# Attention scores: the low part of q against K's high part alone, as two 64-row matmuls on the two halves of the array

## The chip, the cores and the metric

The kernel runs on one core of a Trainium2 chip. The metric is the device time of one execution in microseconds (us). A profile of one execution goes with it: the hardware profiler's records of every instruction on TensorE (PE, and PEld for its weight loads), VectorE (DVE), ScalarE (ACT), GpSimd (POOL) and the queue of DMA issues on SyncE (SP).

## What is computed

The reference is a trunk of two layers over 2048 frames of width 1024: a gated MLP layer (A), then a chunked attention layer (B). The change touches the scores of layer B alone:

```
q, z = split(h @ w_qz);  q = q * 64 ** -0.5         # 16 heads of 64
for each chunk c of 64 queries:                      # keys: its own chunk and 8 before it
    sc = einsum('bqhd,bkhd->bhqk', qc, kc) + bias
    p  = softmax(where(valid, sc, -1e30))
    o  = einsum('bhqk,bkhd->bqhd', p, vc)
x = x + (o * silu(z)) @ w_out
```

## The kernel before

**Numbers in two parts.** TensorE takes the operands in a 32-bit form that it rounds (`F32R`). The kernel keeps the accuracy by writing every operand as a high part plus a low part and adding up products of parts. `mm3` (lines 113 to 116) does this for all projections with three matmuls: high by high (line 114), high by low (115), low by high (116). Each adds 128 rows of contraction into 512 columns.

**Scores.** A head is 64 wide, half of the array's 128 rows, and the kernel before uses the other half for the low part of K. `project(t, p)` makes, for each of the two heads `hd` of a pair `p`, a tile `kx` of 128 partitions and 1024 key columns. Its half `r` holds K's high part (ACT copy, line 1410), its other half `r2` K's low part (DVE subtraction, line 1411). The right 512 columns are the keys of the present stretch `t`. They are stored to `khd` in DRAM (line 1419), and the left 512, the keys of the stretch before, are loaded from there (line 1421). For q there are two tiles, `Qh` (high) and `Ql` (low), each made on one half of the partitions (lines 1397, 1398) and copied to the other half by a DMA (line 1403), so that both halves hold the same values.

`score(t, p, u)` takes 128 queries of one head (`u` counts eight such blocks of a pair, four for each head) against 640 keys, in two segments of 320 columns, each in a PSUM bank of its own. It issues four matmuls of 128 rows (line 1473): `Qh` with segment 0 and segment 1 of `kx`, then `Ql` with both. With `Qh` on both halves the sum over 128 rows is qh·kh + qh·kl, with `Ql` it is ql·kh + ql·kl. In the first stretch, t = 0, there are fewer keys and one segment only.

**Behind a score** come DVE (bias and row minimum, line 1481), ACT (exponential, 1488), DVE (reciprocal, 1491), POOL (scaling, 1492), then `flip`: five transposes on PE (1508), and the split of their result on ACT and DVE (1512, 1513). `value` multiplies by V (1533). `drain` adds the two halves of its result: ACT copies one half into the tile `ot` (1552), DVE adds the other (1553).

**Order.** The sequence is 2048 frames in four stretches `t` of 512, each with eight pairs of heads. In the loop over `u` the scores run two blocks ahead of `flip`; the generator `ahead` feeds in the projections of the next pair (tiles `pj`: q, then k, then the gate) and, from t = 1 on, the output projection of the stretch before (`bo`). What stands in the code is the order of issue that the author asks for. The framework's planner then arranges the instructions of each engine by its own estimates of when operands will be there; `add_manual_dep` (as in `on_beat`, `paced_by_pj`) ties some to others. So an engine's order in the trace need not be that of the code, and DMA issues on SP above all move.

**Buffers.** `ot` has a tag of its own with one buffer. The tag `C` has four buffers of 512 columns: in t = 1, for p below 4, `o_sums` takes four at a time for sums of output weights (tiles `wo`); from t = 1 on the output projection takes them for rows of the residual (`or`, `oc`, `jk`).

Of the kernel before, what the change touches and what calls it, by code (L numbers as in the profile page):

```python
# [9 lines left out]
F32 = mybir.dt.float32  # L10
F32R = mybir.dt.float32r
# [6 lines left out]
P = 128  # L18
# [3 lines left out]
T = 512  # L22
# [11 lines left out]
def trunk_kernel(  # L34
# [20 lines left out]
    nc = tc.nc  # L55
# [15 lines left out]
    khd = [  # L71
        [dram.tile([2, P, T], F32, name=f"khd{t}_{p}") for p in range(NPAIR)]
        for t in range(NT - 1)
    ]
# [163 lines left out]
    def keep_all():  # L238
        while kept:
            nc.sync.dma_start(*kept.pop(0))  # L240
# [1113 lines left out]
    with ExitStack() as bctx:  # L1354
        cb = bctx.enter_context(tc.tile_pool(name="cb", bufs=1, reuse_waits="tile"))
        sb = bctx.enter_context(tc.tile_pool(name="sb", bufs=2, reuse_waits="tile"))
# [5 lines left out]

        vtl = {}
        kt = {}
        qt = {}
        zt = {}

        def halves(hd):
            return slice(hd * 64, hd * 64 + 64), slice(64 - hd * 64, 128 - hd * 64)

        def half_tile(tag, name, bufs, dtype=F32):
            return sb.tile([P, 512], dtype, tag=tag, name=name, bufs=bufs)
# [17 lines left out]
        def project(t, p):  # L1390
            for acc in one(t, p, 1):
                yield
            for hd in range(2):
                qh = sb.tile([P, T], F32R, tag="Q", name=f"Qh{t}_{p}_{hd}", bufs=8)
                ql = sb.tile([P, T], F32R, tag="Q", name=f"Ql{t}_{p}_{hd}", bufs=8)
                r, r2 = halves(hd)
                nc.scalar.mul(qh[r, :], acc[r, :], 0.125)
                nc.vector.scalar_tensor_tensor(
                    ql[r, :], acc[r, :], 0.125, qh[r, :].bitcast(F32),
                    op0=ALU.mult, op1=ALU.subtract,  # L1400
                )
                for x_ in (qh, ql):
                    nc.sync.dma_start(x_[r2, :].bitcast(F32), x_[r, :].bitcast(F32))
                qt[t, p, hd] = (qh, ql)
            for acc in one(t, p, 0):
                yield
            for hd in range(2):
                r, r2 = halves(hd)
                kx = sb.tile([P, 2 * T], F32R, tag="K", name=f"K{t}_{p}_{hd}", bufs=4)
                nc.scalar.copy(kx[r, T:], acc[r, :])  # L1410
                nc.vector.tensor_tensor(
                    kx[r2, T:], acc[r, :], kx[r, T:].bitcast(F32), op=ALU.subtract
                )
                if t + 1 < NT:
                    k_store = (khd[t][p][hd], kx[:, T:].bitcast(F32))
                    if held:
                        kept.append(k_store)
                    else:
                        nc.sync.dma_start(*k_store)
                if t > 0:  # L1420
                    nc.sync.dma_start(kx[:, :T].bitcast(F32), khd[t - 1][p][hd])
                kt[t, p, hd] = kx
            if not held:
                keep_all()
# [33 lines left out]
        def score(t, p, u):  # L1458

            hd, qb = divmod(u, 4)  # L1460
            h = 2 * p + hd
            if qb == 1 and (h + 1 < NH or t + 1 < NT):
                load_bias(t + (h + 1) // NH, (h + 1) % NH)
            bias = bias_t[t, h]
            kx = kt[t, p, hd]
            c0 = 0 if t > 0 else 512 - qb * P
            n = 640 - c0
            koff = qb * P + c0
            ps = pss.tile([P, 2, 512], F32, tag="ss", name=f"s{t}_{h}_{qb}")
            nseg, w = (2, 320) if n == 640 else (1, n)  # L1470
            for i, q in enumerate(qt[t, p, hd]):
                for sg in range(nseg):
                    mm(  # L1473
                        ps[:, sg, :w], q[:, qb * P : (qb + 1) * P],
                        kx[:, koff + sg * w : koff + (sg + 1) * w],
                        start=i == 0, stop=i == 1,
                    )
            pr = sb.tile([P, 640], F32, tag="Pr", name=f"pr{t}_{h}_{qb}", bufs=4)
            ns = sm.tile([P, 2], F32, tag="ns", name=f"ns{t}_{h}_{qb}", bufs=4)
            nm, sl = ns[:, 0:1], ns[:, 1:2]  # L1480
            nc.vector.tensor_tensor_reduce(  # L1481
                out=pr[:, c0:].rearrange("p (a b) -> p a b", a=nseg),
                in0=ps[:, :nseg, :w],
                in1=bias[:, c0:].rearrange("p (a b) -> p a b", a=nseg),
                scale=-1.0, scalar=3.0e38, op0=ALU.add, op1=ALU.min,
                accum_out=nm,
            )
            nc.scalar.activation(  # L1488
                pr[:, c0:], pr[:, c0:], AF.Exp, scale=-1.0, bias=nm, accum_out=sl
            )  # L1490
            nc.vector.reciprocal(sl, sl)  # L1491
            nc.gpsimd.tensor_scalar(  # L1492
                pr[:, c0:], pr[:, c0:], sl, 1.0, op0=ALU.mult, op1=ALU.mult
            )
            prs[t, h, qb] = pr
# [49 lines left out]
        def drain(t, p, hd, po):  # L1545
            h = 2 * p + hd
            if hd == 0:
                og32s[t, p] = sb.tile([P, T], F32, tag="og32", name=f"og32_{t}_{p}", bufs=2)
            og32 = og32s[t, p]
            r, r2 = halves(hd)  # L1550
            ot = sb.tile([P, T], F32, tag="ot", name=f"ot{t}_{h}", bufs=1)
            nc.scalar.copy(ot[r, :], po[r2, :])
            nc.vector.tensor_tensor(og32[r, :], po[r, :], ot[r, :], op=ALU.add)
            if hd == 0:
                return
            if hd == 1 and t + 1 == NT and p >= 6:
                last_og(p, og32, zt[t, p])
            elif hd == 1:
                og = sb.tile([P, T], F32, tag="og", name=f"og{t}_{p}", bufs=2)
                nc.vector.scalar_tensor_tensor(  # L1560
                    og[:], og32[:], 0.5, zt[t, p][:], op0=ALU.mult, op1=ALU.mult
                )
                o4 = og[:].rearrange("p (j r s) -> p r j s", j=2, r=2)
                for r_ in range(2):
                    nc.sync.dma_start(ogd[t][:, r_, p], o4[:, r_])
# [383 lines left out]
        def steps_of(t, p):  # L1949
            n = 24  # L1950
            if p + 1 < NPAIR:
                n = 16 + 8 * len(GATES[t][p])
            elif t + 1 == NT:
                n = 13
            return n + SHARE[t][p]
# [12 lines left out]
        for t in range(NT):  # L1968
            for p in range(NPAIR):
                gen = ahead(t, p) if t + p else first  # L1970
                total = steps_of(t, p) - (0 if t + p else 8)
                per = 11 if p + 1 == NPAIR and t + 1 < NT else 16
                todo = []
                if t + 1 == NT and p + 1 == NPAIR:
                    o_early[t - 1, 3] = o_right(t - 1)(3)
                    todo = last_open()
                if t == 1 and p < 4:
                    todo = o_sums(p, lambda n: half_tile("C", n, 4), lambda n: half_tile(
                        "S", n, 4, F32R
                    ))  # L1980
                if (t, p) == (0, 3):
                    nc.sync.dma_start(gf[:], fin_g.partition_broadcast(P))
                done = 0
                for u in range(8):
                    if u < 6:
                        score(t, p, u + 2)
                    elif p + 1 < NPAIR or t + 1 < NT:
                        score(t + (p + 1) // NPAIR, (p + 1) % NPAIR, u - 6)
                    upto = total * (2 * u + 1) // per
                    take(gen, upto - done)  # L1990
                    done = max(done, upto)
                    if u == 4:
                        value(t, p, 0)
                    elif u == 0 and before:
                        value(*before, 1)
                    flip(t, p, u)
                    drain_all()
                    send_all()
                    square_all()
                    if u and finals:  # L2000
                        finals.pop(0)()
                    if todo:
                        todo.pop(0)()
                    upto = total * (2 * u + 2) // per
                    take(gen, upto - done)
                    done = max(done, upto)
                if t + 1 < NT or p + 1 < NPAIR:
                    run(gen)
                before = t, p
# [62 lines left out]
```

## Time and profile before

| | us |
|---|---|
| median of 3 runs | 2642.36 |
| lowest and highest | 2638.15, 2643.76 |
| the profiled execution, its own time | 2642.95 |
| its span (first to last instruction) | 2641.2 |
| first score matmul | 1527.6 after the start |

How to read it: a row of grouped instructions gives line, engine, operation, the tile written and those read, the shape, the count, then after the bar the time in which at least one was running, the mean duration in ns of one, and the idle time of the engine ahead of them with what ended it. A `LDWEIGHTS` puts the stationary operand into the array, a `MATMUL` streams the moving one. Matmuls are pipelined: the record of one lasts longer than the distance to the next, so rates are read from starts, not from durations. A row of the timeline gives start, duration, engine, line, operation, tiles, shape and how many like it follow each other.

### The profile page before, as it was taken

Reading aid. Unit: us, or ns where it says so; the run is one execution under the profiler, and the core shown is the slowest. Engines: PE = TensorE matmul, PEld = TensorE weight load, DVE = VectorE, ACT = ScalarE, POOL = GpSimd, SP = SyncE. Lnnn points to the kernel's source line nnn. Section 1 sums busy time; section 2 is a strip of 40 time slices with the busy share of each in tenths; the row PEclk is TensorE's granted clock in tenths of the full one; section 3 lists DMA queues with packets and bytes.
Section 4 is the critical chain, followed back from the end, with each engine's and each line's share of the span. In section 5 each row is a group of like instructions: output and inputs, shape, how many; then the busy total and the mean of one; then the engine's idle time right before and its main releaser. Section 6 shows DMA issues by size and latency. Waiting matters only on the chain. (4 is left out here: it accounts for less than half of the span.)

```text
span 2641.2 us, 37945 instructions
## 1 busy us (share of the span) xinstructions
PE 2583.6 (98%) x12752; PEld 2154.9 (82%) x12752; DVE 1933.1 (73%) x3040; ACT 1411.7 (53%) x2511; POOL 901.8 (34%) x875
## 2 busy tenths in 40 slices
PE   9999999999999999999989999999999999999997
PEld 7788788778888888888878778888888888888886
DVE  5984796776768667757776767778778777877677
ACT  7553373553644535333355456666656655666564
POOL 3802254152252413104134334344332322332245
PEclk9999999999999999999999999999999999999999
DMA  8899978988888869858776587778787666775667
GB/s 315 292 349 339 367 270 337 325 304 311 316 333 300 318 225 339 320 199 283 259 263 211 188 270 234 229 241 266 247 277 261 222 208 218 255 228 160 195 229 248
DMA packets 276162, 709.82 MB, mean 269 GB/s; under 512 B 29184, under 2 KB 69120, under 8 KB 275968
## 3 DMA queue, kind: packets, MB, share of 16 engines
q1 hardware_dynamic: 275968, 707.40, 77.6%
q8 instruction: 102, 1.67, 0.2%
q14 instruction: 92, 0.75, 0.1%
HBM read 520.11 MB, written 176.69 MB: 264 GB/s over the span
## 5 line engine op out<-in xcount | busy, mean ns | idle before, releaser
L114 PE MATMUL P<-T,S 128*128 128x512 f32 x1248 | 494.6, 396 | 14.1 <-DVE x L597 6.7
L116 PE MATMUL P<-T,S 128*128 128x512 f32 x1248 | 487.8, 391 | 0.0
L115 PE MATMUL P<-T,S 128*128 128x512 f32 x1248 | 487.3, 390 | 0.3 <-DVE T L522 0.3
L1492 POOL TENSOR_SCALAR pr<-pr,ns 128x640 f32<-128x640 f32 (+4 forms) x256 | 206.8, 808 | 534.2 <-DVE ns L1491 445.9
L114 PE MATMUL pj<-hh_b,wh_b 128*128 128x512 f32 x768 | 319.7, 416 | 0.2 <-ACT wh_b L231 0.2
L116 PE MATMUL pj<-hh_b,wl_b 128*128 128x512 f32 x768 | 303.8, 396 | 0.8 <-DVE wl_b L232 0.8
L115 PE MATMUL pj<-hl_b,wh_b 128*128 128x512 f32 x768 | 302.5, 394 | 0.0
L1488 ACT ACTIVATE pr<-pr,ns 128x640 f32<-128x640 f32 (+4 forms) x256 | 195.5, 764 | 194.6 <-DVE ns L1481 193.7
L114 PEld LDWEIGHTS P<-T,S 128*128 128x128 f32 x1248 | 234.6, 188 | 65.2 <-DVE x L597 6.2
L116 PEld LDWEIGHTS P<-T,S 128*128 128x128 f32 x1248 | 234.6, 188 | 50.8 <-DVE S L441 0.4
L115 PEld LDWEIGHTS P<-T,S 128*128 128x128 f32 x1248 | 234.9, 188 | 44.7 <-DVE T L522 0.6
L1513 DVE TENSOR_TENSOR pt<-tp,pt 128x640 fp32r<-128x640 f32 (+4 forms) x256 | 188.3, 736 | 43.9 <-ACT pt L1512 41.3
L1481 DVE CUSTOM_DVE_ANT_0 pr<-s,bias 128x640 f32<-128x640 f32 (+4 forms) x256 | 187.9, 734 | 36.2 <-PE s L1473 29.7
L1512 ACT CAST pt<-tp 128x640 fp32r<-128x640 f32 (+4 forms) x256 | 158.7, 620 | 53.7 <-PE tp L1508 49.6
L1508 PE MATMUL tp<-ident,pr 128*128 128x128 f32 x1120 | 166.6, 275 | 10.7 <-DVE pt L1513 8.2
L116 PEld LDWEIGHTS pj<-hh_b,wl_b 128*128 128x128 f32 x768 | 144.5, 188 | 35.4 <-DVE wl_b L232 2.9
L1508 PEld LDWEIGHTS tp<-ident,pr 128*128 128x128 f32 x1120 | 130.5, 141 | 46.1 <-issue 17.5
L114 PEld LDWEIGHTS pj<-hh_b,wh_b 128*128 128x128 f32 x768 | 145.4, 189 | 18.1 <-ACT wh_b L231 1.8
L1533 PEld LDWEIGHTS pv<-pt,V 128*128 128x128 f32 x896 | 142.8, 188 | 21.2 <-DVE pt L1513 4.5
L115 PEld LDWEIGHTS pj<-hl_b,wh_b 128*128 128x128 f32 x768 | 145.4, 189 | 16.2 <-DVE hl_b L189 0.2
L1533 PE MATMUL pv<-pt,V 128*128 128x256 f32 (+3 forms) x896 | 154.2, 319 | 2.4 <-DVE pt L1513 1.2
L232 DVE TENSOR_TENSOR wl_b<-raw_b,wh_b 128x1024 fp32r<-128x1024 f32 x96 | 120.5, 1257 | 28.8 <-ACT wh_b L231 27.9
(300 smaller groups left out, 5855.7 us busy)
## 6 DMA issues: line engine op xcount, KB each, us to landing
S<-hsd SPq DMA_DIRECT2D x224, 512.0 KB, 5.7
rw<-in_w_a SPq DMA_DIRECT2D x108, 512.0 KB, 6.3
A<-ytd SPq DMA_DIRECT2D x72, 512.0 KB, 5.8
raw_b<-wk SPq DMA_DIRECT2D x72, 512.0 KB, 4.2
hsd<-S SPq DMA_DIRECT2D x56, 512.0 KB, 6.0
V<-vhd SPq DMA_DIRECT2D x56, 512.0 KB, 5.5
bias<-reld SPq DMA_DIRECT2D x64, 320.0 KB, 4.1
va<-vd SPq DMA_DIRECT2D x32, 512.0 KB, 6.2
```

The lines of the kernel that those rows point to most:

```text
L114: first = mm(ps, lh, rh, start=first, stop=False)
L115: mm(ps, lh, rl, start=False, stop=False)
L116: mm(ps, ll, rh, start=False, stop=last)
L232: tv(wl[:], raw[:], wh[:].bitcast(F32), op=sub)
L1481: nc.vector.tensor_tensor_reduce(out=pr[:, c0:].rearrange("p (a b) -> p a b", a=nseg), in0=ps[:, :nseg, :w], in1=bias[:, c0:].rearrange("p ...
L1488: nc.scalar.activation(pr[:, c0:], pr[:, c0:], AF.Exp, scale=-1.0, bias=nm, accum_out=sl)
L1492: nc.gpsimd.tensor_scalar(pr[:, c0:], pr[:, c0:], sl, 1.0, op0=ALU.mult, op1=ALU.mult)
L1508: ins = tpose(tp[:, b, :], pr[:, b * P : (b + 1) * P], ident[:])
L1512: nc.scalar.copy(oh, tp[:, b0:5, :].rearrange("p a b -> p (a b)"))
L1513: nc.vector.tensor_tensor(pt[:, 2560 + o + b0 * P : 2560 + o + 640], tp[:, b0:5, :].rearrange("p a b -> p (a b)"), oh.bitcast(F32), op=ALU ...
L1533: mm(po[:, q0 * P : q1 * P], vtl[t, p][:, i, hs], rhs, start=(i == blocks[0] and j == 0), stop=(i == 7 and j == 1),)
```

## The change

`Ql` meets only K's high part: the product ql·kl is dropped, and the contraction of the `Ql` matmuls goes from 128 rows to 64. For t above 0, segment 0 runs on the half `r` of the array, where `kx` holds the high part, and segment 1 on the half `r2`. For that a second tile `K2` (one buffer for the whole kernel; head 0 uses one half of its partitions, head 1 the other) gets K's high part copied to the half `r2`, by two DMAs for each head: one from `kx`, one from `khd`. For head 0 they are issued in `project`, for head 1 at the start of the next pair's loop. `Qh` is as before, and so is t = 0. To make room, `ot` goes into the tag `C`.

```
         k2t = {}
         k2s = []
         second = []
...
                 if t > 0:
                     nc.sync.dma_start(kx[:, :T].bitcast(F32), khd[t - 1][p][hd])
+                    if not k2s:
+                        k2s.append(sb.tile([P, 2 * T], F32R, name="K2", bufs=1))
+                    k2 = k2t[t, p] = k2s[0]
+
+                    def again(k2=k2, kx=kx, r=r, r2=r2, src=khd[t - 1][p][hd]):
+                        nc.sync.dma_start(k2[r2, T:].bitcast(F32), kx[r, T:].bitcast(F32))
+                        nc.sync.dma_start(k2[r2, :T].bitcast(F32), src[r])
+
+                    if hd:
+                        second.append(again)
+                    else:
+                        again()
...
             for i, q in enumerate(qt[t, p, hd]):
                 for sg in range(nseg):
+                    rows, src = slice(0, P), kx
+                    if i and t > 0:
+                        rows, src = halves(hd)[sg], (kx, k2t[t, p])[sg]
                     mm(
-                        ps[:, sg, :w], q[:, qb * P : (qb + 1) * P],
-                        kx[:, koff + sg * w : koff + (sg + 1) * w],
+                        ps[:, sg, :w], q[rows, qb * P : (qb + 1) * P],
+                        src[rows, koff + sg * w : koff + (sg + 1) * w],
                         start=i == 0, stop=i == 1,
                     )
...
-            ot = sb.tile([P, T], F32, tag="ot", name=f"ot{t}_{h}", bufs=1)
+            ot = sb.tile([P, T], F32, tag="C", name=f"ot{t}_{h}", bufs=4)
...
                 done = 0
+                while second:
+                    second.pop(0)()
                 for u in range(8):
```

More of the change, by code (lines that the diff above doesn't have):

```diff
@@ L1364, in trunk_kernel @@
         kt = {}
+        k2t = {}
+        k2s = []
+        second = []
         qt = {}
```

## The prediction

> **What bounds the kernel now.** I read the page first: the busy shares, then the chain of waits that ended last.
>
> ```profile
> span 2641.2 us, 37945 instructions
> PE 2583.6 (98%) x12752; PEld 2154.9 (82%) x12752; DVE 1933.1 (73%) x3040; ACT 1411.7 (53%) x2511; POOL 901.8 (34%) x875
> PE 33%; DVE 5%; DMA 2%; issue 1%; POOL 1%; ACT 1%; SPq 0%; DVEq 0%; POOLq 0%; ACTq 0%
> PE pj L116 6%; PE pj L114 6%; PE pj L115 6%; PE pv L1533 5%; PE s L1473 4%; PE tp L1508 4%; PE bo L115 1%; PE bo L116 1%; PE bo L114 1%; DVE pt L1513 1%; DVE pr L1481 1%; DVE y L1831 1%; DVE wl_b L232 0%; DMA or<-x1d 0%; POOL raw_b L216 0%
> ```
>
> The chain accounts for 43% of the span, roughly the attention stage, which fills the last 1113 us. In it 33 of 43 parts are PE, and the scores (s L1473) have 4%, some 106 us. The view of windows confirms this for the three stretches t = 1, 2, 3; its columns after the length are busy time and count for PE, PEld, DVE, ACT and POOL, then clock, DMA share and GB/s.
>
> ```profile
> 1725.00:2012.00 287.00, 285.61 (x1566) 244.52 (x1565) 224.55 (x403) 185.48 (x333) 108.29 (x132) 1.00 0.80 263
> 2012.00:2303.00 291.00, 288.33 (x1579) 247.01 (x1578) 220.33 (x398) 177.15 (x317) 86.46 (x119) 1.00 0.70 226
> 2303.00:2590.00 287.00, 281.21 (x1543) 239.63 (x1542) 217.65 (x391) 172.88 (x312) 98.95 (x124) 1.00 0.65 208
> ```
>
> PE runs over 98% of each stretch at the full granted clock; DVE, next, stands at 78% or less. What PE is spared here comes off the end, nearly whole. What it is made to wait goes onto it.
>
> **The matmuls that change.** From the groups by line and shape:
>
> ```profile
> L1473 PE MATMUL s<-K,Qh 128*128 128x320 f32 x384 | 89.3, 313 | 1.3 <-DVE ns L1481 1.2
> L1473 PE MATMUL s<-K,Ql 128*128 128x320 f32 x384 | 88.0, 308 | 0.0
> ```
>
> 384 `Ql` matmuls are 192 scores of two (three stretches, eight pairs, eight blocks). Their rate is in the starts of PE's timeline:
>
> ```profile
> 1999.95 0.45 PE L1473 MATMUL s<-K,Qh 128*128 128x320 f32 x2
> 2000.24 0.46 PE L1473 MATMUL s<-K,Ql 128*128 128x320 f32 x2
> 2000.53 0.39 PE L114 MATMUL pj<-hh_b,wh_b 128*128 128x512 f32 x1
> 2000.76 0.40 PE L115 MATMUL pj<-hl_b,wh_b 128*128 128x512 f32 x1
> 2001.00 0.39 PE L116 MATMUL pj<-hh_b,wl_b 128*128 128x512 f32 x1
> 2001.23 0.40 PE L114 MATMUL pj<-hh_b,wh_b 128*128 128x512 f32 x1
> 2001.46 0.39 PE L115 MATMUL pj<-hl_b,wh_b 128*128 128x512 f32 x1
> 2001.69 2.35 PE L1533 MATMUL pv<-pt,V 128*128 128x512 f32 x13
> 2004.29 0.50 PE L116 MATMUL pj<-hh_b,wl_b 128*128 128x512 f32 x1 [0.25 <-DVE wl_b L232]
> ```
>
> The two `Ql` matmuls hold PE from 2000.24 to 2000.53: 0.29 us, 0.146 each. So all of them cost 192 x 0.292 = 56 us, and this is all that the change can touch. Fewer rows by themselves save nothing: time goes with the 320 columns, and those stay. The gain exists only if the two 64-row matmuls, on different halves of the array, run at the same time. Every row of PE in this trace has the shape `128*128`, so nothing here shows that, and it has to be bounded.
>
> - Full overlap: one 0.146 of the two disappears, 192 x 0.146 = 28.0 us.
> - None: 0.
> - Limited by the weight loads. Each of the two needs its own load of 128 columns. The transposes show how closely loads can follow each other, since their matmuls are short (128 columns) and the loads set their pace:
>
> ```profile
> 1787.94 0.71 PE L1508 MATMUL tp<-ident,pr 128*128 128x128 f32 x5
> L1508 PE MATMUL tp<-ident,pr 128*128 128x128 f32 x1120 | 166.6, 275 | 10.7 <-DVE pt L1513 8.2
> ```
>
> Five take 0.71 us and one lasts 0.275, so they start (0.71 - 0.275) / 4 = 0.109 us apart. Count from the start of the second `Qh` matmul. Two loads in turn are done at 0.218; the second `Ql` matmul streams until 0.218 + 0.146 = 0.364, where the next full-height matmul can begin. Today that point is 3 x 0.146 = 0.438. The gain is 0.074 for each score, 192 x 0.074 = 14.2 us.
>
> I take 14.2: the load pace is the nearest row, though a load of half the rows could be quicker. The Trainium skill, "TensorE: Matmul & The Clock Gate", section "LDWEIGHTS (loading the stationary operand)", says that the time of a load goes by columns and not by rows, which would make 0.109 hold for 64 rows as well.
>
> **The copy of K.** `K2` adds two DMAs for each head from t = 1 on, 96 in all, of 64 x 512 x 4 bytes each, 12.6 MB beside the 709.8 MB of the page. Their twin is the copy of `Qh` and `Ql` to the other half (line 1403), same size:
>
> ```profile
> L1403 SPq DMA_DIRECT2D Ql<-Ql x64: 461/467/1331, 1520.1 to 2539.6; - x64
> DMA to landing us min/median/max: 2.2/3.8/8.1
> ```
>
> Issuing takes 96 x 0.467 = 45 us of SP over 865 us, and the DMA engines are at 0.65 to 0.80. I cost the traffic itself at nothing; the cover is that PE waits for the `Q` copies only three times in all (rows below). What matters is when the first score of a pair needs `K2`. In t = 1 that is at once:
>
> ```profile
> 1784.85 0.58 ACT L1410 CAST K<-pj 64x512 fp32r<-64x512 f32 x1 [1.14 <-PE pj L116]
> 1785.46 0.69 DVE L1411 TENSOR_TENSOR K<-pj,K 64x512 fp32r<-64x512 f32 x1 [0.15 <-ACT K L1410]
> 1786.17 0.32 SPq L1419 DMA_DIRECT2D khd<-K  x1
> 1786.66 0.45 PE L1473 MATMUL s<-K,Qh 128*128 128x320 f32 x2
> 1786.95 0.46 PE L1473 MATMUL s<-K,Ql 128*128 128x320 f32 x2
> ```
>
> K's high part is ready at 1785.43. A copy issued then lands at 1785.43 + 3.8 = 1789.2, and the second `Ql` matmul would start at 1787.10: 2.1 us early. PE takes its matmuls in order, so everything queued behind, the gate's projection first, would wait. The number of such places is that of the pairs at which PE reaches the score as soon as K is split:
>
> ```profile
>   DVE K L1411: 3.0, 7
>   DMA Qh<-Qh: 2.6, 1
>   DMA Ql<-Ql: 0.6, 2
> ```
>
> Seven places. If nothing fills the waits they cost 7 x 2.1 = 14.7 us. But the planner orders PE by when it believes operands arrive: in the timeline above, 13 `pv` matmuls stand between lines 115 and 116 of one `mm3`, because `wl_b` came late, and only 0.25 us of idle time was left. It knows of the `K2` copies too and will put gate matmuls ahead of that score. What it misjudges stays; today that is 3.0 / 7 = 0.43 us at each such place. I take as much again, 7 x 0.43 = 3.0 us, with 0 and 14.7 as ends. For other pairs there is room:
>
> ```profile
> 2147.72 0.58 ACT L1410 CAST K<-pj 64x512 fp32r<-64x512 f32 x1 [1.16 <-PE pj L116]
> 2156.86 0.46 PE L1473 MATMUL s<-K,Ql 128*128 128x320 f32 x2
> ```
>
> The copy could land at 2152.1, the `Ql` pair starts at 2156.86. For head 1 the copies go out at the start of the pair's loop, two blocks of `u` before its first score. The wait of the copy for ACT on SP holds up what is behind it there (K's store of head 1, the bias, the next raw weights) no longer than the store of line 1419 does, which waits for the later DVE result; in t = 3, where there is no store, it is new, by the 0.58 us of the ACT copy: nothing.
>
> **`ot` in the tag C.** While `o_sums` holds all four buffers (t = 1, four pairs), a drain may have to wait for one, with `pv`'s PSUM bank held meanwhile. There are four banks of that tag, and `pj` fills one in 24 x 0.232 = 5.6 us (spacing of the lines 114 to 116 above) and is read by four operations of 0.58 to 0.69 (the ACT and DVE rows above), 2.5 us, so two serve it and PE is covered. I cost it at nothing. With the cover gone, PE would wait for a combination of weights on POOL in four places. A gain has no place here: the drains of one pair lie a whole half-loop apart and do not contend for the one buffer.
>
> **Sum.** 2642.95 us is the profiled execution's own time (1.75 us lie outside its span); the median is 0.6 below. From the median: 2642.4 - 14.2 + 3.0 = 2631.2 us, a gain of 0.42%. A difference under 0.2% (5.3 us) could not be told from none.
>
> **Rivals.**
>
> *Changing the shape costs a wait (slower).* PE would go from 128 rows to 64 and back in each score. If a new shape may only start when the array is empty, each change waits out what is still in flight: a `Ql` record lasts 0.308 us, its successor starts after 0.146, so 0.162. The loads fit under that wait. From the second `Qh` start to the next full-height matmul it then takes 2 x 0.308 = 0.616 instead of 0.438: 0.178 more, 192 x 0.178 = 34.2 us, with the 3.0 a time of 2679.6. It decides from 0.146 / 2 = 0.073 us for each change, where even full overlap is eaten up. For it: the distance between a record's end and the next start shows work in flight that a change of wiring would have to respect. Against it: fp32 transposes and rounded matmuls alternate in the trace without such a gap, but those share one shape. The Trainium skill, "TensorEngine Tiling (Array Packing)", section "Tiling Modes", states that changing the tiling mode drains TensorE; by that rule this rival is the outcome, and no run so far shows it. If the weight loads must wait as well, two more spacings of 0.109 come in: 0.396 x 192 = 76 us, beyond my range.
>
> *The halves take turns (no change).* The change then does not do what it is for: 2642.4 + 3.0 = 2645.4. Nothing in the trace speaks for or against it.
>
> *The copies come late and nothing fills in.* 2642.4 - 14.2 + 14.7 = 2642.9. For it: the seven places; against it: how rarely PE waits for a DMA today.
>
> **How the numbers follow.** The forecast (the halves overlap, the change of shape is free) gets 0.45. Its own range reaches from 2614 (full overlap and no waits) to 2636 (only 33/43 of 14.2 reaching the end, and 5 us of waits): 0.43 faster, 0.02 same. The wait on changing shape gets 0.33, for lack of any row against it: 0.29 slower, 0.04 same (a short wait). Taking turns 0.11: 0.06 same, 0.05 slower. Late copies 0.11: 0.02 faster, 0.05 same, 0.04 slower. Sums: faster 0.45, same 0.17, slower 0.38. Cases of both signs carry weight, so the range goes from full overlap with the 3.0 us of waits (2617.4, taken as 2616) to 2684, just past the first rival; what lies outside is mainly the drained loads.
>
> **What would show it.** Right: `Ql` rows of 64 rows; in a pair the second starts about 0.07 to 0.11 us after the first, and the next `pj` about 0.36 after the second `Qh`; all else in PE's groups unchanged; waits of `s` for `K2` of a few us in t = 1. The first rival: over 0.3 us from the second `Qh` to the first `Ql`, and again behind the pair. Taking turns: 0.146 between the two. Late copies: a wait of `s` for `K2` near 15 us. Wrong altogether: the time moves in rows that the change does not touch, such as `bo` or `tp` waiting for buffers of tag C.

## The result and the profile after

The change makes the kernel slower: a median of 2684.6 us against 2643.1, a ratio of 1.0155 (95% interval 1.0137 to 1.0172), some 41 us. The forecast of 2631.2 has the wrong sign. The first rival, in which the change of shape costs a wait, gave 2679.6.

The page after the change, its span, the engines and the chain:

```profile
span 2680.6 us, 38102 instructions
PE 2631.1 (98%) x12752; PEld 2139.9 (80%) x12752; DVE 1930.3 (72%) x3040; ACT 1413.5 (53%) x2511; POOL 904.2 (34%) x875
PE 36%; DVE 3%; DMA 2%; issue 1%; POOL 1%; ACT 1%; SPq 0%; DVEq 0%; POOLq 0%; ACTq 0%
```

PE's busy share is 98% as before, and its share of the chain has grown from 33% to 36%. The count of matmuls is the same 12752. The extra time is time that matmuls take up, not idle time: PE's busy time grew by 47.5 us and the span by 39.4. The groups of PE by line and shape after the change, then those of its weight loads, two rows before and the same two after (before, the row of the `Ql` loads holds those of t = 0 too):

```profile
L1491 PE MATMUL s<-K,Qh 128*128 128x320 f32 x384 | 88.9, 311 | 1.3 <-DVE ns L1499 1.0 <-DVE K L1414 0.3
L1491 PE MATMUL s<-K,Ql 64*128 64x320 f32 x384 | 84.5, 409 | 0.3 <-DMA K<-K 0.3
```

```profile
L1473 PEld LDWEIGHTS s<-K,Ql 128*128 128x128 f32 x448 | 76.6, 188 | 2.9 <-DMA Ql<-Ql 0.4
L114 PEld LDWEIGHTS pj<-hh_b,wh_b 128*128 128x128 f32 x768 | 145.4, 189 | 18.1 <-ACT wh_b L231 1.8
```

```profile
L1491 PEld LDWEIGHTS s<-K,Ql 64*128 64x128 f32 x384 | 38.1, 183 | 41.4 <-issue 41.0 <-DMA K<-K 0.4
L114 PEld LDWEIGHTS pj<-hh_b,wh_b 128*128 128x128 f32 x768 | 144.7, 188 | 40.7 <-issue 21.5 <-ACT wh_b L231 1.6 <-ACT Sho L340 0.3
```

The `Ql` matmuls have the new shape `64*128` and their records grew from 308 to 409 ns. The 384 loads cover 38.1 us of time where each lasts 0.183: 384 x 0.183 = 70 us in all, so they run two at a time. Ahead of them the load path stands idle for 41.0 us "issue", which means that nothing the profile shows held it up: 41.0 / 192 = 0.21 us for each score. The load of the next projection has 21.5 us of the same kind. Before, neither row shows any. One score after the change in the timeline (start, duration, engine; the last bracket is idle time):

```profile
1999.67 0.41 PEld L1491 LDWEIGHTS s<-K,Qh 128*128 128x128 f32 x2
1999.89 0.45 PE L1491 MATMUL s<-K,Qh 128*128 128x320 f32 x2
2000.27 0.19 PEld L1491 LDWEIGHTS s<-K,Ql 64*128 64x128 f32 x2 [0.19 <-issue]
2000.28 0.41 PE L1491 MATMUL s<-K,Ql 64*128 64x320 f32 x2
2000.62 0.19 PEld L114 LDWEIGHTS pj<-hh_b,wh_b 128*128 128x128 f32 x1 [0.15 <-issue]
2000.62 0.50 PE L114 MATMUL pj<-hh_b,wh_b 128*128 128x512 f32 x1
...
2000.96 0.39 PE L115 MATMUL pj<-hl_b,wh_b 128*128 128x512 f32 x1
```

Two loads last 0.19 together and two matmuls 0.41 together: the halves do run side by side, loads included. But the load of `Qh` starts at 1999.67, well ahead of its matmul at 1999.89, while the load of `Ql` and its matmul start together, and so do those of `wh_b`. At both changes of shape the load starts only 0.09 us after the point where inside one shape the next matmul would start (table below), and nothing hides it. I call these 0.09 us "emptying". That the array empties in them is a reading and no record: the ends of matmuls are modelled, and the second `Qh` record still runs for 0.07 us after the load of `Ql` has started (1999.89 + 0.45 = 2000.34 against 2000.27).

From the starts of all scores whose records can be followed, 192 before and 191 after, as medians:

| from, to | before, ns | after, ns |
|---|---|---|
| second `Qh` to first `Ql` | 147 | 239 |
| first to second `Ql` | 147 | 3 |
| second `Ql` to the next matmul | 146 | 340 |
| that one (`pj`) to its successor | 231 | 335 |
| second `Qh` to that successor | 669 | 917 |

Each score takes 0.248 us more, 192 x 0.248 = 47.6 us. The account: the overlap takes away 0.144. Entering costs 0.092 of emptying and a load, which is counted in the next step but one (340 - 146 = 194 holds that load, about 0.104, and another emptying of about 0.090; the same-half kernel below shows the two apart). Leaving exposes a load of 335 - 231 = 0.104. So a change of shape costs about 0.093 + 0.104 = 0.197 us, two of them 0.394.

The loss builds up evenly, as it should if every score pays. The first score of a pair starts, before and after, at 1725.6 and 1721.6 us (t = 1, pair 0), 2012.8 and 2024.3 (t = 2), 2303.6 and 2329.9 (t = 3), 2552.1 and 2591.7 (t = 3, pair 7): 43.6 us over 184 scores, 0.237 each.

### The profile page after: what moved, and what is told of

Read it like the earlier page. It is cut to its first block, busy times and chain, and to the rows that moved or that the text cites. A ratio compares the mean times of both kernels' runs of the same rounds, so it can differ in the third digit from the quotient of the medians.

```text
span 2680.6 us, 38102 instructions
## 1 busy us (share of the span) xinstructions
PE 2631.1 (98%) x12752; PEld 2139.9 (80%) x12752; DVE 1930.3 (72%) x3040; ACT 1413.5 (53%) x2511; POOL 904.2 (34%) x875
## 5 line engine op out<-in xcount | busy, mean ns | idle before, releaser
L114 PE MATMUL pj<-hh_b,wh_b 128*128 128x512 f32 x768 | 333.3, 434 | 0.6 <-ACT wh_b L231 0.6
L114 PEld LDWEIGHTS pj<-hh_b,wh_b 128*128 128x128 f32 x768 | 144.7, 188 | 40.7 <-issue 21.5
```

The source lines that it names most:

```text
L114: first = mm(ps, lh, rh, start=first, stop=False)
```

## The experiments

The theory: each change between 128 and 64 rows costs an emptying and an exposed weight load, 0.197 us, whatever is done in between. The rivals: 64-row matmuls are slow in themselves or the price goes with each pair; the copies of K or the shared buffers cost the time; any change in the number of rows does it. In the diffs below, lines removed are those of the kernel named.

**Same half, no copies.** From the kernel before:

```
+                    rows = halves(hd)[0] if i and t > 0 else slice(0, P)
                     mm(
-                        ps[:, sg, :w], q[:, qb * P : (qb + 1) * P],
-                        kx[:, koff + sg * w : koff + (sg + 1) * w],
+                        ps[:, sg, :w], q[rows, qb * P : (qb + 1) * P],
+                        kx[rows, koff + sg * w : koff + (sg + 1) * w],
```

> The kernel before with the low q matmuls cut to the 64 rows of K's high part, both segments on the same half of the array, without K2 and its copies and with ot as before. Theory (each change between 128 and 64 rows costs about 0.197 us: 0.093 until the array is empty and 0.104 for a weight load that nothing hides; side by side saves 0.146): two changes and no overlap, 192 x 0.394 = 76 us more than before, 2719; some of it may be absorbed in waits that exist today, so 2705 to 2720. The two low matmuls start 0.146 us apart. Rival, the 64-row matmul is slow in itself (its load is never hidden): the two also start 0.25 us or more apart, and 2735 or more. Rival, the copies of K are the cause: no copies here, 2643.

Measured 2705.9 us, ratio 1.0239 (1.0220 to 1.0259), 63 us more. Its timeline:

```profile
2003.44 0.45 PE L1474 MATMUL s<-K,Qh 128*128 128x320 f32 x2
2003.82 0.30 PEld L1474 LDWEIGHTS s<-K,Ql 64*128 64x128 f32 x2 [0.19 <-issue]
2003.83 0.56 PE L1474 MATMUL s<-K,Ql 64*128 64x320 f32 x2
2004.31 0.19 PEld L114 LDWEIGHTS bo<-wh_bo,Sho 128*128 128x128 f32 x1 [0.19 <-issue]
2004.31 0.50 PE L114 MATMUL bo<-wh_bo,Sho 128*128 128x512 f32 x1
2004.42 0.19 PEld L115 LDWEIGHTS bo<-wl_bo,Sho 128*128 128x128 f32 x1
2004.65 0.40 PE L115 MATMUL bo<-wl_bo,Sho 128*128 128x512 f32 x1
```

The loss is there without K2 and without any of its copies, so the copies are not its cause. The medians are 238, 252, 235 and 337 ns for the first four steps of the table above. I expected 146 between the two `Ql` matmuls, and 252 is what I had written for the rival. The reason is in the rows: the first record starts with its load, so its load is counted in that gap. The second load is hidden, since second `Ql` to next is 235 = 146 + 89 and not 340. The second `Qh` to the successor is 1062 ns, against 669 before: 0.393 us, the same price as above without the overlap, 192 x 0.393 = 75 us, of which 63 reach the end.

**The copies and buffers alone.** From the changed kernel, with the four matmuls of the kernel before; K2 is written and not read.

```
-                    rows, src = slice(0, P), kx
-                    if i and t > 0:
-                        rows, src = halves(hd)[sg], (kx, k2t[t, p])[sg]
                     mm(
-                        ps[:, sg, :w], q[rows, qb * P : (qb + 1) * P],
-                        src[rows, koff + sg * w : koff + (sg + 1) * w],
+                        ps[:, sg, :w], q[:, qb * P : (qb + 1) * P],
+                        kx[:, koff + sg * w : koff + (sg + 1) * w],
```

> The changed kernel with all its copies into K2 and ot in tag C, but the four score matmuls with 128 rows as before; K2 is written and never read. Theory (the changes of shape are the cause): 2643, within 6 us. Rival, the copies and the shared buffers cost the time (DMA, the SP queue, the planner's order): most of the 41 us, 2670 to 2685.

Measured 2652.0 us, ratio 1.0032 (1.0022 to 1.0043): 9 us, outside what the theory expected and far from the rival's 27 to 42. The copies and the shared buffers together do cost something. The waits of PE in this kernel between 2160 and 2204 us, then the landing of two DMAs before and here (KB each, median us from issue to landing):

```profile
PE bo L114 <- DMA wh_bo<-ows: 2.1, 1, 2.1
PE bo L115 <- DMA wl_bo<-ows: 0.7, 1, 0.7
```

```profile
wh_bo<-ows SPq DMA_DIRECT2D x24, 512.0 KB, 4.5
wl_bo<-ows SPq DMA_DIRECT2D x24, 512.0 KB, 5.8
```

```profile
wh_bo<-ows SPq DMA_DIRECT2D x24, 512.0 KB, 5.5
wl_bo<-ows SPq DMA_DIRECT2D x24, 512.0 KB, 6.9
```

The weights of the output projection land a microsecond later, and at one place PE waits for them, 2.1 and 0.7 us; from the first score of that pair to the next pair's it takes 40.3 us there and 35.6 in the kernel before. So 4.7 us of the difference lie in this one pair.

**Only the buffer of `ot`.** From the kernel before:

```
-            ot = sb.tile([P, T], F32, tag="ot", name=f"ot{t}_{h}", bufs=1)
+            ot = sb.tile([P, T], F32, tag="C", name=f"ot{t}_{h}", bufs=4)
```

> The kernel before with ot in tag C as the only edit. It tells whether the 9 us that the copies and the shared buffers cost together, with 128-row matmuls, come from the buffers. If the copies are their cause: 2643, within 4 us. If the buffers are: 2649 to 2653.

Measured 2646.8 us, ratio 1.0011 (1.0000 to 1.0022): between nothing and 6 us. By the middle values 3 of the 9 us go with the buffer and 6 with the copies; whether the buffer has any share isn't settled. The copies with `ot` in its old buffer were not run. The landing of the output weights in this kernel:

```profile
wh_bo<-ows SPq DMA_DIRECT2D x24, 512.0 KB, 5.0
wl_bo<-ows SPq DMA_DIRECT2D x24, 512.0 KB, 6.1
```

They land later than before here too, by 0.5 and 0.3 us, without any copies. So not all of that microsecond comes from the copies' traffic. PE's wait of 2.1 us for `wh_bo` is missing here.

**96 rows.** From the same-half kernel:

```
-                    rows = halves(hd)[0] if i and t > 0 else slice(0, P)
+                    rows = slice(0, 96) if i and t > 0 else slice(0, P)
```

> The kernel before with the low q matmuls on partitions 0 to 95 instead of 128, so that a part of the products is left out; no K2. 96 rows still need the whole height of the array. Theory (what costs is switching the array between whole and halves): nothing, 2643 within 6 us. Rival, any change in the number of rows from one matmul to the next empties the array: two changes for each score, 192 x 0.394 = 76 us more, 2705 to 2720.

Measured 2642.6 us, ratio 0.9997 (0.9985 to 1.0008). Group, and one score in the timeline:

```profile
L1474 PE MATMUL s<-K,Ql 96*128 96x320 f32 x384 | 89.3, 312 | 0.0
```

```profile
2007.94 0.45 PE L1474 MATMUL s<-K,Qh 128*128 128x320 f32 x2
2008.23 0.46 PE L1474 MATMUL s<-K,Ql 96*128 96x320 f32 x2
2008.53 0.40 PE L114 MATMUL pj<-hh_b,wh_b 128*128 128x512 f32 x1
```

96 rows instead of 128 cost nothing and save nothing. What costs is going to 64 rows, half the array's height, and back.

**Four changes in a score.** From the changed kernel:

```
-            for i, q in enumerate(qt[t, p, hd]):
-                for sg in range(nseg):
+            qs = qt[t, p, hd]
+            order = [(i, sg) for i in range(2) for sg in range(nseg)]
+            if t > 0:
+                order = [(0, 0), (1, 0), (0, 1), (1, 1)]
+            for i, sg in order:
+                    q = qs[i]
```

> The changed kernel with the score's matmuls in the order high q on segment 0, low q on segment 0, high q on segment 1, low q on segment 1, so that the array changes shape four times in a score instead of twice and the halves never meet. Theory: 4 x 0.197 = 0.788 us more for each score than before, 192 x 0.788 = 151 us, 2760 to 2795. Rival, the cost goes with the pair of 64-row matmuls and not with each change: only the overlap is lost, 2685 + 28 = 2713.

Measured 2774.8 us, ratio 1.0497 (1.0480 to 1.0514), 132 us more. Twice the changes and no overlap cost twice what the same-half kernel lost (63). The rival's 2713 is out.

**The pair twice.** From the changed kernel:

```
-            for i, q in enumerate(qt[t, p, hd]):
+            qh, ql = qt[t, p, hd]
+            for i, q in enumerate((qh, ql, ql) if t > 0 else (qh, ql)):
...
-                        start=i == 0, stop=i == 1,
+                        start=i == 0, stop=i == (2 if t > 0 else 1),
```

> The changed kernel with the 64-row pair of each score issued twice in a row (low q by high K is added twice, so the scores are off by that). Theory (a change of shape costs 0.197 us, inside one shape the halves run side by side at full rate): the second pair adds only its streaming, 0.146 us, 192 x 0.146 = 28 us: 2705 to 2713. Rival, every pair brings its own emptying and unhidden loads: another 0.2 to 0.34 us for each score, 2722 to 2750. Rival, the halves take turns: 56 us, 2741.

Measured 2718.8 us, ratio 1.0275 (1.0258 to 1.0292), 6 us above the theory's upper figure and 3 below the lowest of the first rival's, so the time alone is no clean verdict. The timeline decides:

```profile
2001.35 0.45 PE L1492 MATMUL s<-K,Qh 128*128 128x320 f32 x2
2001.73 0.56 PE L1492 MATMUL s<-K,Ql 64*128 64x320 f32 x4
2002.22 0.50 PE L114 MATMUL bo<-wh_bo,Sho 128*128 128x512 f32 x1
2002.56 0.39 PE L115 MATMUL bo<-wl_bo,Sho 128*128 128x512 f32 x1
```

From the start of the 64-row block to the next matmul it is 0.49 with two pairs and was 0.34 with one: 0.15 for the second pair, its streaming alone. 28 us follow from that; 1.0275 - 1.0155 is 32, within the two intervals.

**Two different pairs.** From the changed kernel, with `Qh` on K's high part only; the product of high q and low K is left out:

```
-                    if i and t > 0:
+                    if t > 0:
```

> The changed kernel with the high q matmuls on 64 rows as well: high q by high K and low q by high K, each as a pair on the two halves; the product of high q and low K is left out. The array changes shape twice in a score as in the changed kernel, but two 128-row matmuls (0.292) become one pair (0.146). Theory: 28 us less than the changed kernel, 2652 to 2660, still above the kernel before although a quarter of the products is missing. Rival, the cost goes with the number of 64-row pairs: 2684 - 56 + 48 to 65, 2676 to 2693.

Measured 2668.7 us, ratio 1.0086 (1.0067 to 1.0104). That lies between the two expectations, 9 us above the theory's. My figure started from the 41 us of the changed kernel; counted from the kernel before, two changes less two matmuls of 0.146 are 0.394 - 0.292 = 0.102, 192 x 0.102 = 20 us, and with up to 9 for the copies 2663 to 2672. The groups show that the second pair pays no change of shape:

```profile
L1491 PE MATMUL s<-K,Qh 64*128 64x320 f32 x384 | 82.5, 411 | 2.0 <-DVE ns L1499 1.0 <-DMA K<-K 1.0
L1491 PE MATMUL s<-K,Ql 64*128 64x320 f32 x384 | 63.3, 308 | 0.0
```

Now `Qh` has the long records, since it enters the shape; `Ql`, coming second, is back at the 308 ns that it had at 128 rows.

**Four pairs, narrow and wide.** The changed kernel with `(qh, ql, ql, ql, ql)` in the loop of the pair-twice kernel, and the kernel before with the same loop:

> The changed kernel with the 64-row pair of each score issued four times in a row (low q by high K is added four times, so the scores are off by that). Theory: one entry and one exit whatever the number of pairs, so three more pairs add 3 x 0.146 = 0.438 us for each score, 192 x 0.438 = 84 us on 2684: 2765 to 2778. With four pairs the 64-row shape should win against four 128-row pairs (the next kernel) by 4 x 0.146 - 0.393 = 0.191 for each score, 37 us, less up to 9 us for the copies: 28 to 37 us. Rival, the cost returns with every pair: another 3 x 0.2, 2880.

> The kernel before with its two 128-row low q matmuls issued four times in a row (the same surplus, with the product of both low parts as well). Six more matmuls of 0.146 us for each score: 192 x 0.876 = 168 us on 2643, 2800 to 2812. It has to come out 28 to 37 us above the kernel with four 64-row pairs if the change of shape is a fixed price that more work in one shape pays back; below it if the price goes with the pair.

Measured 2773.8 us (ratio 1.0491, 1.0464 to 1.0519) for the narrow ones and 2804.5 us (1.0615, 1.0585 to 1.0645) for the wide ones: with four pairs for one entry and one exit the halves win by 31 us. One score of the narrow, then of the wide:

```profile
2006.60 0.85 PE L1492 MATMUL s<-K,Ql 64*128 64x320 f32 x8
2007.38 0.51 PE L114 MATMUL bo<-wh_bo,Sho 128*128 128x512 f32 x1
```

```profile
2007.31 1.33 PE L1474 MATMUL s<-K,Ql 128*128 128x320 f32 x8
2008.48 0.39 PE L114 MATMUL pj<-hh_b,wh_b 128*128 128x512 f32 x1
```

0.78 us to the next matmul against 1.17. The narrow pairs of a score start 0.252, 0.146 and 0.147 us apart (medians): only the first of them shows an exposed load, so a 64-row matmul is not slow in itself. The price and the saving put the point where the shape pays at 0.394 / 0.146 = 2.7 pairs in one block, and the two runs agree with it on the far side; two or three narrow pairs were not compared with as many wide ones. A score has one. Three scores' pairs in one block would need the sums of three scores in PSUM at once, where now there is room for one (two banks, beside four for `pj`, `pv`, `bo` and two for `tp`), and would gain 3 x 0.146 - 0.394 = 0.044 us for three scores, 3 us in all, less than the 9 us that the copies and the shared buffers cost. So no version that beats the kernel before follows from this, and none was run.

## Why the prediction was wrong, point by point

**PE as the bound: right.** What PE is made to wait does reach the end, though not all of it. The same-half kernel shows 63 of 75 us, the one with four changes 132 of 192 x 0.788 = 151. A part of this lies in waits that exist already and shrink; PE's idle time (span less busy time) is 57.6 us before, 49.5 after the change, 48.3 in the same-half kernel and 46.0 in the one with four changes. One such wait is that of the transposes for DVE's work on the buffer ahead, 8.2 us before and 3.7 after the change:

```profile
L1526 PE MATMUL tp<-ident,pr 128*128 128x128 f32 x1120 | 166.7, 274 | 5.5 <-DVE pt L1531 3.7 <-DVE rr_f L1831 0.9 <-POOL pr L1510 0.7
```

Where the other microseconds were absorbed stays open.

**The halves run side by side: right, and mis-sized.** I took 0.074 for each score, limited by loads in turn. The loads run in parallel too, 3 ns apart, so full overlap was the right end: 0.144, 28 us. My reason, the load pace of the transposes, was a rate of full-height loads on one and the same array. So the sign that I named, a second `Ql` 0.07 to 0.11 us after the first, did not come. The Trainium skill, "TensorEngine Tiling (Array Packing)", section "Tiling Modes", says under "Key Properties" that different tiles can do LdWeights and Matmul in parallel; the trace agrees (384 loads of 0.183 us in 38.1 us, matmuls 3 ns apart).

**The change of shape is free: wrong, and this step decided the sign.** The prediction put 0.45 on it and nothing for it into the sum, though no row of the trace showed that it was free, for every matmul had one shape. The price is 0.394 for each score, 192 x 0.394 = 76 us, against 28 us of gain. The rule of the Trainium skill, "TensorEngine Tiling (Array Packing)", section "Tiling Modes", that a change of the tiling mode drains TensorE, was in my hands with a rival beside it, at 0.33. The trace agrees with it in that 0.09 us pass at each change before the next load starts, and 96 rows, which cost nothing, agree with its limit to a change of mode.

**The rival's price: near in sum, off in its terms.** I took 0.162 for emptying the array (the rest of a record after its successor's start) and hid the loads under it. My sign for this rival, over 0.3 us from the second `Qh` to the first `Ql` and again behind the pair, came only behind the pair: 0.239 and 0.340. Emptying takes 0.09, and the load follows it instead of overlapping: 0.10. The two errors, and the overlap that this rival had at full size, left 0.178 against the measured 0.248. That 2679.6 came close to 2684.6 is partly luck. The exposed loads, which I had put beyond my range on top of the long emptying, are half of the price.

**The wait for K2: small, as forecast, but the seven places were misread.** After the change the waits of PE (loads and matmuls) ahead of scores show K's split as before and little for K2:

```profile
  DVE K L1414: 3.0, 8
  DMA K<-K: 0.7, 2
```

I took 3.0 more with 14.7 as the upper end; it is 0.7. Both of my figures came from seven waits of 3.0 us that I took for places from t = 1 on. In the kernel before, only one of them lies in the window 1725 to 2590 us, and it is idle time ahead of a weight load:

```profile
PEld s L1473 <- DVE K L1411: 0.5, 1, 0.5
```

The other six, 2.5 us, lie in t = 0, whose scores the change leaves alone, and none of the seven is a wait ahead of a matmul. With one such place my upper end would have been 2.1 us and not 14.7. That the planner filled the time with other matmuls is the reason I gave, and no run tested it.

**The copies' traffic at nothing: wrong, by up to 9 us together with the buffers.** I looked at who waits for the copies and at nothing else. In the kernel with the copies alone, 4.7 us of the loss lie in one pair, where PE meets output weights that land late. That they are late because they share the DMA engines with the copies is not shown: about a half (0.5 of 1.0 us) and a quarter (0.3 of 1.1) of their delay is there without copies. How much of the 9 us remains in the changed kernel, where PE has other delays, can't be separated from the 41.

**`ot` in tag C: not refuted.** The interval for it alone reaches from 0 to 6 us.

## What to carry to other kernels

Splitting the array pays by the length of the block that stays in one shape, not by the matmul: count the changes of shape, price each at an emptying and an unhidden weight load, and compare with the streaming time saved inside the block. A price for which the trace has no row is not zero; when a written rule names it and the gain is of the same size, the rule's case should be the forecast. And a copy that hardly any matmul waits for is not free by that alone: these, with the buffers shared for them, cost 9 us of 2643.

## What the runs showed of the hardware

- A change between full and half height keeps the next load back by 0.09 us (the "emptying"), after matmuls of 320 and of 512 columns alike: 239 - 147 = 92 ns after `Qh`, and 326 - 231 = 95 ns from `pj` to the first `Qh` in the kernel with two different pairs.
- Loads did not start ahead of their matmul over such a change (41.0 us of idle load path ahead of 384 loads). Inside the new shape they did, even on the half that was streaming: in the same-half kernel the step behind the second `Ql` matmul is 235 ns, 146 and an emptying of 89, with no room for a load.
- A load of 64 rows lasted 183 ns, one of 128 rows 188.
